# The gate of the context's recurrence ahead of the mLSTM half of its output projection, with four load buffers on ScalarE's queue

## The chip, the cores and the metric

The kernel runs on one core of one Trainium2 chip. A core has a matrix engine (TensorE, PE in the profile; PEld is its weight loading), VectorE (DVE), ScalarE (ACT), GpSimd (POOL) and SyncE (SP), which here only issues DMAs; the other engines can issue DMAs too. The metric is the device time of one execution in microseconds (us). The kernel before took 2059.33 us, the median of three runs (2057.45 to 2059.98).

## The reference

Two layers of a backbone over 512 latent tokens and 256 context tokens, width 1024, in f32. The change is in layer 0, whose mixer has two halves of 512 channels with one joint output projection:

```python
def rwkv_run(...):                    # both directions, context first, then latent
    def step(S, inp):                 # per token, 8 heads of 64
        sa = einsum('zbhij,zbhj->zbhi', S, a_t)
        S = S * w_t + sa * b_t + v_t * k_t
        return S, einsum('zbhij,zbhj->zbhi', S, r_t)
...
def rwkv_out(y, r, k, v, g, ...):
    yn = group_norm(y) * ln_w + ln_b
    return (yn + bonus(r, k, v)) * g  # the gate
...
oc = concatenate([mlstm_out(...), rwkv_out(...)]) @ out_w    # context's mixer output
h_ctx = h_ctx + gc1 * oc
h_ctx = h_ctx + gc2 * sq_relu_mlp(modulate(rms_norm(h_ctx), sc2, cc2), w1, w2)
```

The recurrence over the context ends in the state from which the one over the latent tokens starts.

## The kernel before

Activations lie with channels on partitions. A GEMM takes its f32 operands as two fp32r parts each: `xh`, `xl` of the activations (ScalarE casts, L280, VectorE subtracts, L281; `split_x`), `wh`, `wl` of the weights (ScalarE, L237; VectorE or GpSimd, L241), and adds the products xh·wh, xl·wh and xh·wl in one PSUM tile `psg`. One output tile of 128 channels over the 256 context tokens from 512 inputs has 12 matmuls; the result goes into the residual `res_c` on VectorE (L338).

The recurrence runs in 12 steps of 64 tokens, steps 0 to 3 the context and 4 to 11 the latent tokens, each step with its two directions. `step(s)` (L945) is the chain on the state: `psC<-X,AS`, `r`, `psC<-r,T`, `X`, then the new state `psC<-X,BK`, `S`, and the output `psC<-X,Q` and `psC<-S,ar`, which is added into `ya_c`. `pre(s)` (L842) prepares a step: it loads `ar`, `bk`, `AS`, `X` over SP, forms the products `psA`, brings the triangular blocks through DRAM (`dA`, `M`) into a form in which VectorE inverts them (`tm`, `Xi`, 15 pairs of instructions at L889 and L891), and back through DRAM (`invD`, `Xr`, and its transpose `Xt`, L899); from there four small products `psI` with `dd` (L909), `t` (L917, L919) and `d` (L930, ScalarE) lead to `T` (L938). `rwkv_norms` (L1007) normalises `ya_c` once step 3 is through (L995 to L1003).

The large GEMMs lie between these steps. The generator `fillers()` (L1113) gives them out in one order, and `pull` takes so many microseconds of them after each step (`PL`, L1131). Their order here is: the latent half of the input projection, the latent mLSTM half of the output projection, the context's mLSTM half (`ctx_mlstm`, L1042), and, once step 3 has set "ctx", `ctx_half` (L1058): the gate (`rwkv_gate`, L1013), its splits, the context's recurrence half of the output projection and the context's MLP. The gate moves `ya_c` through TensorE into `psy`, multiplies by the first half of `gb` (VectorE, L1023) and adds the second half (GpSimd, L1024) into `ro_c`, four times, for 128 channels each; `gb` comes from DRAM (`gD`) through two buffers. `moD` holds the context's mLSTM output in DRAM, loaded into `xlmc` and split there into `xhmc` and `xlmc`. What an engine runs when is set by a tile scheduler at build time; each engine then keeps its order. `Stats` and `rms` (`psst`, `psbc`, `rs`) form the norm ahead of the MLP, whose split input is `xh`, `xl`.

Of the kernel before, what the change touches and what calls it, by code (L numbers as in the profile page):

```python
# [11 lines left out]
F32 = mybir.dt.float32  # L12
# [6 lines left out]
P = 128  # L19
D = 1024  # L20
NK = D // P
CT = 256
# [95 lines left out]
def hybrid_kernel(ctx: ExitStack, tc: tile.TileContext, A, out):  # L118
    WS = [int(x) for x in "2222"]
    nc = tc.nc  # L120
    uid = [0]

    def nm(s):
        uid[0] += 1
        return f"{s}_{uid[0]}"
# [6 lines left out]
    def mm(o, l, r, start=True, stop=True, shared=False, tile=None):  # L132
        kw = {"tile_position": (32 * tile[0], 32 * tile[1])} if tile else {}
        return nc.tensor.matmul(o, l, r, start=start, stop=stop, skip_group_check=shared, **kw)  # L134
# [109 lines left out]
    def gemm(ap, xs, psp, both=0, k0=0, k1=NK, x0=0):  # L244

        w = split_w(ap[:, P * k0:P * k1], both)
        res = [gemm_w(w, x, psp, x0) for x in xs]
        bg[2] += bg[1]
        while bg[2] >= 1.0:
            bg[2] -= 1.0  # L250
            next(bg[0], None)
        return res
# [26 lines left out]
    def split_x(h, l, x):  # L279
        nc.scalar.copy(h, x)  # L280
        nc.vector.tensor_tensor(l, x, h.bitcast(F32), op=ALU.subtract)  # L281
# [55 lines left out]
    def add_gated(r_, ps, cnd, m, layer, idx):  # L337
        nc.vector.scalar_tensor_tensor(r_, ps, modcol(layer, idx, m, cnd), r_, op0=ALU.mult, op1=ALU.add)  # L338

    def out_proj(layer, cnd, res, x, k0, k1, psp, both, stats=None, x0=None):  # L340

        for m in range(NK):
            add_gated(res[:, m, :], gemm(A["out_w"][layer, m], [x], psp, both, k0, k1, k0 if x0 is None else x0)[0], cnd, m, layer, 2)
            if stats:
                stats.add(res[:, m, :])
            yield x[2] / 512 * 0.65 * (k1 - k0)
# [62 lines left out]
    xin = A["hT"]  # L409
    CTX, LAT = slice(0, CT), slice(CT, T)  # L410
    st_x = [ExitStack() for _ in SEGS]
    XN = [None, None]
    for i in (1, 0):
        n = SEGS[i][1]
# [3 lines left out]
    psg2 = st_f.enter_context(tc.tile_pool(name="psg2", bufs=2, space=PSUM, side="right"))  # L418
# [61 lines left out]
    gD = [pd.tile([P, 2, 4, n], F32, name=f"gD{n}") for _, n, _ in SEGS]  # L480
    moD = pd.tile([P, HM, T], F32, name="moD")
# [20 lines left out]
    with tc.tile_pool(name="pg1", bufs=1) as pg1:  # L502
# [20 lines left out]
        for z in range(2):  # L523
# [5 lines left out]
            m = pg1.tile([HM, T], F32, tag="mz", name=nm("m"))  # L529
# [483 lines left out]
    def rwkv_gate(si, dst, po, psp):  # L1013

        n = SEGS[si][1]
        for p in range(4):
            gb = po.tile([P, 2, n], F32, tag="gb", name=nm("gb"))
            nc.sync.dma_start(gb, gD[si][:, :, p, :])
            py_ = psp.tile([P, n], F32, tag="g", name=nm("psy"))
            for c in range(n // CR):  # L1020
                for q in range(2):
                    mm(py_[hs_[q], 64 * c:64 * c + 64], YA[si][hs_[q], c, p, :], id2[q])
            nc.vector.tensor_tensor(gb[:, 0], py_, gb[:, 0], op=ALU.mult)  # L1023
            nc.gpsimd.tensor_tensor(dst(p), gb[:, 0], gb[:, 1], op=ALU.add)  # L1024
# [5 lines left out]
    def lat_mlstm(res):  # L1030

        with tc.tile_pool(name="prm", bufs=1, side="right") as prm:
            xh = prm.tile([P, 4, LT], F32R, name="xhom")
            xl = prm.tile([P, 4, LT], F32R, name="xlom")
            for i in range(4):
                y = xl[:, i, :].bitcast(F32)
                nc.sync.dma_start(y, moD[:, i, LAT])
                split_x(xh[:, i, :], xl[:, i, :], y)
            for m in range(NK):
                nc.sync.dma_start(res[:, m, :], xin[:, m, LAT])  # L1040
            yield from out_proj(0, 0, res, (xh, xl, LT), 0, 4, psg2, WS[2])

    def ctx_mlstm():

        pres = st_c.enter_context(tc.tile_pool(name="pres", bufs=1, side="right"))
        res = RES["c"] = pres.tile([P, NK, CT], F32, name="res_c")
        wide[0] = st_w.enter_context(tc.tile_pool(name="wp2", bufs=1, side="right"))
        nc.sync.dma_start(res, xin[:, :, CTX])
        with tc.tile_pool(name="pcm", bufs=1, side="right") as pcm:
            xh = pcm.tile([P, 4, CT], F32R, name="xhmc")  # L1050
            xl = pcm.tile([P, 4, CT], F32R, name="xlmc")
            y = xl.bitcast(F32)
            nc.sync.dma_start(y, moD[:, :, CTX])
            split_x(xh, xl, y)
            yield from out_proj(0, 1, res, (xh, xl, CT), 0, 4, psg2, WS[2])

    def ctx_half():
        res = RES["c"]  # L1058
        with tc.tile_pool(name="pro", bufs=1, side="right") as pro, tc.tile_pool(name="po", bufs=2, side="right") as po:
            ro = pro.tile([P, 4, CT], F32, name="ro_c")  # L1060
            rwkv_gate(0, lambda p: ro[:, p, :], po, psg2)
            xh = pro.tile([P, 4, CT], F32R, name="xhoc")
            xl = pro.tile([P, 4, CT], F32R, name="xloc")
            for i in range(4):
                split_x(xh[:, i, :], xl[:, i, :], ro[:, i, :])
            stats = Stats(CT, po, psh2, "h")
            yield from out_proj(0, 1, res, (xh, xl, CT), 4, NK, psg2, WS[3], stats, 0)
            rb = stats.rms(psg2, "g")
        yield from mlp(0, 1, CT, res, 8, psg2, "right", WS[3], rb, 0)
        wide[0] = None  # L1070
        st_w.close()
# [45 lines left out]
    def fillers():  # L1117
        yield from rwkv_in(1, psg2, psh2, "h", st_x[1].close)
        done.add("in")
        RES["l"] = st_l.enter_context(tc.tile_pool(name="plr", bufs=1, side="right")).tile([P, NK, LT], F32, name="res_l")  # L1120
        yield from lat_mlstm(RES["l"])
        YA[1] = st_c.enter_context(tc.tile_pool(name="pyl", bufs=1, side="right")).tile([P, 8, 4, 64], F32, name="ya_l")
        done.add("lat")
        yield from ctx_mlstm()
        while "ctx" not in done:
            yield None
        yield from ctx_half()

    fill = fillers()
    PL = [18, 15, 21, 10, 21]  # L1130
    pull(fill, PL[0])  # L1131
# [18 lines left out]
    res = RES["l"]  # L1150
# [11 lines left out]
    with tc.tile_pool(name="prl", bufs=1) as prl, tc.tile_pool(name="pol", bufs=2) as pol:  # L1162
        ro = prl.tile([P, 4, LT], F32, name="ro_l")
        xh = prl.tile([P, 4, LT], F32R, name="xhol")
        xl = prl.tile([P, 4, LT], F32R, name="xlol")
        rwkv_gate(1, lambda p: ro[:, p, :], pol, psg3)
        pull(fill, 1e9)
        st_f.close()
        psg4 = st_q.enter_context(tc.tile_pool(name="psg4", bufs=2, space=PSUM, side="right"))
        psa3 = st_3.enter_context(tc.tile_pool(name="psa3", bufs=1, space=PSUM, side="right"))  # L1170
        for i in range(4):
            split_x(xh[:, i, :], xl[:, i, :], ro[:, i, :])
        stats = Stats(LT, pol, psg3)
        for _ in out_proj(0, 0, res, (xh, xl, LT), 4, NK, psg3, 0, stats, 0):
            pass
        rb = stats.rms()
# [15 lines left out]
    xh = px.tile([P, NK, LT], F32R, name="xh1")  # L1192
    xl = px.tile([P, NK, LT], F32R, name="xl1")
# [290 lines left out]
```

## Time and profile before

| | us |
|---|---|
| median of three runs | 2059.33 |
| lowest, highest | 2057.45, 2059.98 |
| the profiled execution | 2055.02 |
| its span | 2053.2 |
| TensorE busy | 1947.8 (95%) |
| VectorE, ScalarE, GpSimd busy | 1083.9, 874.3, 835.6 |

The mean granted clock of TensorE in this execution was 0.973. All times below are from the span's start. One execution is profiled; the time outside the span (1.8 us) is start and end. A timeline row has its start, how long it took, the line of the kernel, and in brackets how long the engine had been idle and what ended that. The clock of a stretch is given as a share of full speed: 1.00 is 2.4 GHz, 0.50 is 1.2 GHz.

### The profile page before, as it was taken

Reading aid. Unit: us, or ns where it says so; the run is one execution under the profiler, and the core shown is the slowest. Engines: PE = TensorE matmul, PEld = TensorE weight load, DVE = VectorE, ACT = ScalarE, POOL = GpSimd, SP = SyncE. Lnnn points to the kernel's source line nnn. Section 1 sums busy time; section 2 is a strip of 40 time slices with the busy share of each in tenths; the row PEclk is TensorE's granted clock in tenths of the full one; section 3 lists DMA queues with packets and bytes.
Section 4 is the critical chain, followed back from the end, with each engine's and each line's share of the span. In section 5 each row is a group of like instructions: output and inputs, shape, how many; then the busy total and the mean of one; then the engine's idle time right before and its main releaser. Section 6 shows DMA issues by size and latency. Waiting matters only on the chain. (4 is left out here: it accounts for less than half of the span.)

```text
span 2053.2 us, 36769 instructions
## 1 busy us (share of the span) xinstructions
PE 1947.8 (95%) x14924; PEld 1599.5 (78%) x14924; DVE 1083.9 (53%) x2087; ACT 874.3 (43%) x1441; POOL 835.6 (41%) x563
## 2 busy tenths in 40 slices
PE   6899998898897999999999999999999999999998
PEld 4788886666676899889787888888666678888887
DVE  6773645777878666776642221263666664122122
ACT  4444445354533444443433232343665654233232
POOL 1455555233432222224344444434454453444444
PEclk9999999998998999999999999999999999999999
DMA  7356557454585555544524332334111122333232
GB/s 303 107 197 218 176 203 263 123 152 111 166 249 152 124 171 159 146 134 135 210 93 133 94 101 93 101 111 141 59 52 34 57 75 82 103 94 102 93 103 72
DMA packets 171833, 271.62 MB, mean 132 GB/s; under 512 B 74960, under 2 KB 113488, under 8 KB 166544
## 3 DMA queue, kind: packets, MB, share of 16 engines
q1 hardware_dynamic: 166608, 263.76, 41.0%
q10 hardware_dynamic: 5056, 5.51, 0.8%
q8 instruction: 118, 1.93, 0.4%
q14 instruction: 51, 0.42, 0.1%
HBM read 244.06 MB, written 25.17 MB: 131 GB/s over the span
## 5 line engine op out<-in xcount | busy, mean ns | idle before, releaser
L241 POOL TENSOR_TENSOR wl<-w,wh 128x1024 fp32r<-128x1024 f32 (+3 forms) x252 | 573.5, 2278 | 851.5 <-PE psg L134 420.5
L237 ACT CAST wh<-w 128x1024 fp32r<-128x1024 f32 (+3 forms) x319 | 313.4, 985 | 517.5 <-PE psg L134 442.8
L134 PE MATMUL psg<-xh,wh 128*128 128x512 f32 (+1 forms) x1440 | 498.2, 361 | 13.3 <-DVE tm L889 6.5
L134 PE MATMUL psg<-xl,wh 128*128 128x512 f32 (+1 forms) x1440 | 496.5, 357 | 0.8 <-DVE xl L335 0.4
L134 PEld LDWEIGHTS psg<-xh,wh 128*128 128x128 f32 x1440 | 272.3, 190 | 68.3 <-issue 20.5
L134 PE MATMUL psg<-xh,wl 128*128 128x512 f32 (+1 forms) x1440 | 325.0, 356 | 0.0
L134 PEld LDWEIGHTS psg<-xl,wh 128*128 128x128 f32 x1440 | 274.4, 191 | 46.0 <-issue 7.6
L134 PEld LDWEIGHTS psg<-xh,wl 128*128 128x128 f32 x1440 | 242.0, 191 | 41.5 <-issue 7.0
L134 PE MATMUL psg<-hl,wh 128*128 128x512 f32 (+1 forms) x800 | 267.4, 348 | 0.9 <-DVE hl L281 0.9
L134 PE MATMUL psg<-hh,wh 128*128 128x512 f32 (+1 forms) x800 | 266.2, 349 | 1.2 <-DVE res_c L338 1.0
L338 DVE SCALAR_TENSOR_TENSOR res_l<-psg,mod,res_l 128x512 f32<-128x512 f32 (+1 forms) x108 | 74.1, 689 | 277.2 <-PE psg L134 277.2
L134 PEld LDWEIGHTS psg<-hh,wh 128*128 128x128 f32 x800 | 150.9, 189 | 22.5 <-issue 2.0
L134 PEld LDWEIGHTS psg<-hl,wh 128*128 128x128 f32 x800 | 151.2, 189 | 20.6 <-DVE hl L281 1.3
L134 PE MATMUL psg<-hh,wl 128*128 128x512 f32 (+1 forms) x800 | 164.6, 347 | 0.0
L383 DVE TENSOR_SCALAR r<-psg 128x512 f32<-128x512 f32 (+1 forms) x96 | 57.4, 600 | 176.9 <-PE psg L134 176.9
L134 PEld LDWEIGHTS psg<-hh,wl 128*128 128x128 f32 x800 | 131.6, 189 | 19.0
L281 DVE TENSOR_TENSOR hl<-r,hh 128x512 fp32r<-128x512 f32 (+1 forms) x96 | 90.0, 940 | 83.6 <-ACT hh L280 83.4
L384 ACT ACTIVATE r<-r 128x512 f32<-128x512 f32 (+1 forms) x96 | 53.5, 560 | 118.7 <-DVE r L383 118.7
L241 DVE TENSOR_TENSOR wl<-w,wh 128x1024 fp32r<-128x1024 f32 (+1 forms) x67 | 81.5, 1217 | 19.5 <-ACT wh L237 12.0
L889 DVE TENSOR_TENSOR tm<-M,Xi 64x15 f32<-64x15 f32 (+4 forms) x180 | 60.1, 334 | 23.5 <-DMA M<-dA 17.4
L134 PE MATMUL psada<-adaw,sc 128*32 128x256 f32 (+1 forms) x896 | 62.4, 383 | 8.3 <-DMA adaw<-in_ada_w_dram 4.2
L134 PE MATMUL psA<-ar,bk 64*128 64x128 f32 x384 | 55.2, 311 | 8.1 <-issue 3.6
(420 smaller groups left out, 2869.1 us busy)
## 6 DMA issues: line engine op xcount, KB each, us to landing
w<-in_w_dram SPq DMA_DIRECT2D x192, 512.0 KB, 3.6
adaw<-in_ada_w_dram SPq DMA_DIRECT2D x40, 1024.0 KB, 7.2
w<-in_ev_in_dram SPq DMA_DIRECT2D x47, 512.0 KB, 3.7
w<-in_od_in_dram SPq DMA_DIRECT2D x32, 512.0 KB, 3.6
adaw<-in_ada_dram SPq DMA_DIRECT2D x16, 512.0 KB, 11.2
w<-in_out_w_dram SPq DMA_DIRECT2D x32, 256.0 KB, 3.0
bk<-bkD SPq DMA_DIRECT2D x12, 512.0 KB, 4.7
ar<-arD SPq DMA_DIRECT2D x12, 512.0 KB, 4.8
```

Source lines behind the costliest of these rows:

```text
L134: return nc.tensor.matmul(o, l, r, start=start, stop=stop, skip_group_check=shared, **kw)
L237: nc.scalar.copy(wh, w)
L241: eng.tensor_tensor(wl, w, wh.bitcast(F32), op=ALU.subtract)
L281: nc.vector.tensor_tensor(l, x, h.bitcast(F32), op=ALU.subtract)
L338: nc.vector.scalar_tensor_tensor(r_, ps, modcol(layer, idx, m, cnd), r_, op0=ALU.mult, op1=ALU.add)
L383: nc.vector.tensor_scalar(r_, ps, 0.0, None, op0=ALU.max)
L384: nc.scalar.activation(r_, r_, AF.Square)
L889: nc.vector.tensor_tensor(t_, M[:, m:16, j:j + 1].to_broadcast([64, n, m]), Xi[:, j:j + 1, 0:m].to_broadcast([64, n, m]), op=ALU.mult)
```

## The change

`ctx_half` is now a generator `ctx_gate` in three parts. `ctx_mlstm` takes its first part ahead of its own loads: the four `gb` loads, each with a buffer of its own, issued by ScalarE. Then come the loads of `moD`, in four parts and on ScalarE's queue, each split by itself, and `res_c` in two loads on SP. The second part is the gate and the splits of its result, then the mLSTM half of the output projection, then the third part, the rest of what `ctx_half` was. `fillers()` waits for "ctx" ahead of all this, not between.

```diff
--- before.py
+++ after.py
@@ -1014,8 +1014,11 @@
 
         n = SEGS[si][1]
         for p in range(4):
-            gb = po.tile([P, 2, n], F32, tag="gb", name=nm("gb"))
-            nc.sync.dma_start(gb, gD[si][:, :, p, :])
+            if isinstance(po, list):
+                gb = po[p]
+            else:
+                gb = po.tile([P, 2, n], F32, tag="gb", name=nm("gb"))
+                nc.sync.dma_start(gb, gD[si][:, :, p, :])
             py_ = psp.tile([P, n], F32, tag="g", name=nm("psy"))
             for c in range(n // CR):
                 for q in range(2):
@@ -1045,24 +1048,36 @@
         pres = st_c.enter_context(tc.tile_pool(name="pres", bufs=1, side="right"))
         res = RES["c"] = pres.tile([P, NK, CT], F32, name="res_c")
         wide[0] = st_w.enter_context(tc.tile_pool(name="wp2", bufs=1, side="right"))
-        nc.sync.dma_start(res, xin[:, :, CTX])
+        gate = ctx_gate()
+        next(gate)
         with tc.tile_pool(name="pcm", bufs=1, side="right") as pcm:
             xh = pcm.tile([P, 4, CT], F32R, name="xhmc")
             xl = pcm.tile([P, 4, CT], F32R, name="xlmc")
             y = xl.bitcast(F32)
-            nc.sync.dma_start(y, moD[:, :, CTX])
-            split_x(xh, xl, y)
+            for i in range(4):
+                nc.scalar.dma_start(y[:, i, :], moD[:, i, CTX])
+                split_x(xh[:, i, :], xl[:, i, :], y[:, i, :])
+            for m in range(0, NK, 4):
+                nc.sync.dma_start(res[:, m:m + 4, :], xin[:, m:m + 4, CTX])
+            next(gate)
             yield from out_proj(0, 1, res, (xh, xl, CT), 0, 4, psg2, WS[2])
-
-    def ctx_half():
+        yield from gate
+
+    def ctx_gate():
+
         res = RES["c"]
         with tc.tile_pool(name="pro", bufs=1, side="right") as pro, tc.tile_pool(name="po", bufs=2, side="right") as po:
             ro = pro.tile([P, 4, CT], F32, name="ro_c")
-            rwkv_gate(0, lambda p: ro[:, p, :], po, psg2)
             xh = pro.tile([P, 4, CT], F32R, name="xhoc")
             xl = pro.tile([P, 4, CT], F32R, name="xloc")
+            gbs = [po.tile([P, 2, CT], F32, tag="gb", bufs=4, name=nm("gb")) for _ in range(4)]
+            for p in range(4):
+                nc.scalar.dma_start(gbs[p], gD[0][:, :, p, :])
+            yield 0.0
+            rwkv_gate(0, lambda p: ro[:, p, :], gbs, psg2)
             for i in range(4):
                 split_x(xh[:, i, :], xl[:, i, :], ro[:, i, :])
+            yield 0.0
             stats = Stats(CT, po, psh2, "h")
             yield from out_proj(0, 1, res, (xh, xl, CT), 4, NK, psg2, WS[3], stats, 0)
             rb = stats.rms(psg2, "g")
@@ -1121,10 +1136,9 @@
         yield from lat_mlstm(RES["l"])
         YA[1] = st_c.enter_context(tc.tile_pool(name="pyl", bufs=1, side="right")).tile([P, 8, 4, 64], F32, name="ya_l")
         done.add("lat")
-        yield from ctx_mlstm()
         while "ctx" not in done:
             yield None
-        yield from ctx_half()
+        yield from ctx_mlstm()
 
     fill = fillers()
     PL = [18, 15, 21, 10, 21]
```

In the order of TensorE's instructions the first place is the end of the latent mLSTM projection (`psg` from `xhom`). Before, this stands there; `psI` is the preparation of step 3, `xhmc` belongs to the context's mLSTM half, `psA` prepares step 4:

```order
L134 MATMUL psI_5956<-t_1060_5951,AB_5776 32x32 x16
L134 MATMUL psg_6708<-xhmc,wh_6704 128x256
L134 MATMUL psg_6708<-xlmc,wh_6704 128x256
...
L134 MATMUL psg_6708<-xhmc,wl_6706 128x256 x4
L134 MATMUL psA_6370<-ar_6359,bk_6360 128x128 x4
L134 MATMUL psA_6378<-ar_6359,bk_6360 128x128
L134 MATMUL psI_5975<-t_1059_5948,d_1063_5973 32x32 x16
```

and now, up to the first of the context's mLSTM GEMMs (`psy` is the gate, `psC` step 3 up to `psC_6314`, then step 4):

```order
L134 MATMUL psI_5956<-t_1060_5951,AB_5776 32x32 x16
L134 MATMUL psA_6370<-ar_6359,bk_6360 128x128 x4
L134 MATMUL psA_6378<-ar_6359,bk_6360 128x128 x4
L134 MATMUL psI_5975<-t_1059_5948,d_1063_5973 32x32 x16
...
L134 MATMUL psC_6314<-S_5722,ar_5772 64x64 x16
L134 MATMUL psC_6902<-X_6253,AS_6362 64x64 x16
L134 MATMUL psy_6729<-cst,ya_c 64x64 x8
L134 MATMUL psy_6740<-cst,ya_c 64x64 x8
L134 MATMUL psA_7008<-ar_6997,bk_6998 128x128 x4
...
L134 MATMUL psA_7024<-ar_6997,bk_6998 128x128 x4
L134 MATMUL psg_6787<-xhmc,wh_6783 128x256
```

The eight mLSTM GEMMs, which were spread over step 3 and the preparation behind it, have moved behind all of step 3 and behind the gate's `psy`.

The second place is ScalarE's order from the last weight cast of the latent projection to `d` of step 3, before and now in one piece:

```order
 L237 CAST wh_6663<-w_6661 128x512
+L1075 DMA gb_6702<-gD_583 128x2x256
+L1075 DMA gb_6703<-gD_583 128x2x256
+L1075 DMA gb_6704<-gD_583 128x2x256
 L923 ACTIVATE T_5953<-t_1059_5948,cst 128x8x32 x2
-L237 CAST wh_6704<-w_6702 128x512
-L280 CAST xhmc<-xlmc 128x1024
...
+L1075 DMA gb_6705<-gD_583 128x2x256
+L1058 DMA xlmc<-moD 128x256 x4
+L237 CAST wh_6783<-w_6781 128x512
...
 L930 COPY d_1063_5973<-psI_5956 128x128
```

Eight DMA issues have come ahead of `d`, and the split of `xlmc` has gone behind it.

The third place is TensorE behind the last gate GEMM of the context (`psg` from `xhoc`), up to the norm's `psbc`. Before, the rest of step 4 stood there (`psC_6842` to `psC_6883`), and step 5's `psI` with `Xr` came nine matmuls of the MLP later:

```order
L134 MATMUL psg_7418<-xhoc,wl_7416 128x256 x4
L134 MATMUL psC_6842<-r_6840,T_6540 64x64 x16
L134 MATMUL psst_7250<-cst,acc_7272 128x1 x2
L134 MATMUL psC_6861<-X_6253,BK_6416 64x64
L134 MATMUL psst_7250<-cst,sq_7432 128x1 x2
L134 MATMUL psC_6861<-X_6253,BK_6416 64x64 x15
L134 MATMUL psC_6883<-X_6253,Q_6361 64x64 x16
L134 MATMUL psC_6883<-S_6309,ar_6359 64x64 x16
L134 MATMUL psbc_7441<-cst,rs_7438 128x128 x2
```

and now:

```order
L134 MATMUL psI_7105<-Xr_7101,AB_7001 32x32 x16
L134 MATMUL psI_7105<-Xt_7103,AB_7001 32x32 x16
L134 MATMUL psg_7428<-xloc,wh_7424 128x256
L134 MATMUL psg_7428<-xhoc,wl_7426 128x256 x4
L134 MATMUL psC_7610<-X_6901,AS_7000 64x64 x12
L134 MATMUL psst_7260<-cst,acc_7282 128x1 x2
...
L134 MATMUL psI_7140<-Xt_7103,dd_7138 32x32 x16
...
L134 MATMUL psA_7716<-ar_7705,bk_7706 128x128 x4
...
L134 MATMUL psI_7181<-t_1234_7176,AB_7001 32x32 x16
L134 MATMUL psbc_7451<-cst,rs_7448 128x128 x2
```

Step 4 has gone ahead of the last gate GEMM, and the first three `psI` of step 5 and half its successor's `psA` have come ahead of `psbc`.

## Rows read from the trace of the kernel before

**Rows 1.** Windows: stretch, length, busy us of PE, PEld, DVE, ACT, POOL; clock, DMA.
```profile
589.94:639.24 49.30, 40.40 (x532) 36.56 (x521) 35.75 (x90) 18.84 (x37) 10.04 (x12) 0.83 0.69 197
649.94:680.00 30.06, 23.80 (x355) 20.74 (x355) 22.28 (x56) 10.57 (x22) 4.11 (x4) 0.72 0.44 107
639.24:649.94 10.70, 10.31 (x198) 9.72 (x198) 10.52 (x29) 6.63 (x13) 4.02 (x3) 1.00 0.67 203
```

**Rows 2.** Timeline of PE: start, duration, line, output<-inputs, count, [idle before, releaser].
```profile
588.57 1.07 PE L134 MATMUL psg<-xhom,wl 128*128 128x512 f32 x4
589.57 0.45 PE L134 MATMUL psI<-t,AB 32*32 32x32 f32 x32
591.96 0.38 PE L134 MATMUL psg<-xhmc,wh 128*128 128x256 f32 x1 [1.94 <-ACT xhmc L280]
...
597.33 0.45 PE L134 MATMUL psI<-t,d 32*32 32x32 f32 x32
...
598.80 0.28 PE L134 MATMUL psg<-xlmc,wh 128*128 128x256 f32 x1
598.92 0.28 PE L134 MATMUL psg<-xhmc,wh 128*128 128x256 f32 x1
```

**Rows 3.** Timeline of PE, the gate and the projection behind it.
```profile
633.80 0.55 PE L134 MATMUL psg<-xhoc,wh 128*128 128x256 f32 x1 [4.42 <-issue]
...
638.78 0.48 PE L134 MATMUL psI<-Xt,AB 32*32 32x32 f32 x32
...
649.88 0.64 PE L134 MATMUL psg<-xhoc,wl 128*128 128x256 f32 x4
```

**Rows 4.** Timeline of DVE, context norm, triangular inverses and gate.
```profile
611.88 0.41 DVE L889 TENSOR_TENSOR tm<-M,Xi 64x15 f32<-64x15 f32 x1 [0.93 <-DMA M<-dA]
...
614.39 0.67 DVE L1003 TENSOR_TENSOR ya_c<-ya_c,ms 128x512 f32<-128x512 f32 x1
...
630.28 0.17 DVE L891 TENSOR_TENSOR Xi<-Xi,tm 64x15 f32<-64x15 f32 x1
633.27 0.42 DVE L1023 TENSOR_TENSOR gb<-psy,gb 128x256 f32<-128x256 f32 x1 [2.83 <-DMA gb<-gD]
...
638.43 0.17 DVE L889 TENSOR_TENSOR tm<-M,Xi 64x15 f32<-64x15 f32 x1
...
661.42 0.17 DVE L891 TENSOR_TENSOR Xi<-Xi,tm 64x15 f32<-64x15 f32 x1
...
670.22 0.45 DVE L899 STREAM_TRANSPOSE Xt<-Xr 128x256 f32<-128x256 f32 x1 [1.47 <-DMA Xr<-invD]
```

**Rows 5.** Instructions of tile gb: duration ns min/median/max, starts; time to landing.
```profile
L1018 SPq DMA_DIRECT2D gb<-gD x4: 572/632/1118, 590.9 to 629.1; - x4
...
DMA to landing us min/median/max: 5.3/6.4/7.6
```

**Rows 6.** Timeline of PE: the same 16 psA at the two clocks.
```profile
483.17 3.09 PE L134 MATMUL psA<-ar,bk 64*128 64x128 f32 x16
...
615.33 1.71 PE L134 MATMUL psA<-ar,bk 64*128 64x128 f32 x16
```

**Rows 7.** Timeline of ScalarE before step 3's solve.
```profile
586.09 0.62 ACT L237 CAST wh<-w 128x512 fp32r<-128x512 f32 x1
...
592.86 0.25 ACT L930 COPY d<-psI 128x128 f32<-128x128 f32 x1
```

**Rows 8.** Timeline of PE from step 4's solve to step 5.
```profile
652.08 1.15 PE L134 MATMUL psC<-r,T 64*64 64x64 f32 x32 [1.56 <-DVE T L938]
...
657.44 1.86 PE L134 MATMUL psC<-X,BK 128*64 128x64 f32 x29 [1.58 <-DVE X L960]
...
662.31 0.71 PE L134 MATMUL psbc<-cst,rs 128*128 128x128 f32 x4
...
668.53 2.08 PE L134 MATMUL psA<-ar,bk 64*128 64x128 f32 x10 [1.48 <-DMA ar<-arD]
...
698.06 1.15 PE L134 MATMUL psC<-S,ar 64*64 64x64 f32 x32
```

## The prediction

> **What bounds the kernel now.** I read the windows first, because the page's shares are averages. From the end of the latent mLSTM projection to the end of the context's output projection, TensorE is not one long busy stretch [rows 1]: in 589.94:639.24 it works 40.40 of 49.30 us at a mean clock of 0.83, in 639.24:649.94 nearly all the time at 1.00, and in 649.94:680.00 23.80 of 30.06 us at 0.72. So 8.9 and 6.3 us are idle. At clock 0.83 some 8.4 us of the first stretch are missing (0.17 x 49.3), of which about 1.5 fall into idle time; likewise 8.4 less 1.8 in the last. Altogether the two stretches lose about 8.9 + 6.9 = 16 us and 6.3 + 6.6 = 13 us. Everywhere else TensorE is full and later work only shifts, so the change is priced by when TensorE gets through this region.
>
> Then TensorE's timeline. The last latent GEMM begins its tail at 588.57; after the `psI` at 589.57 the engine waits 1.94 us for ScalarE's split of `xlmc` [rows 2]. Eight mLSTM GEMMs of the context (12 matmuls each, 0.12 us apart at the full clock [rows 2], so 1.44 us) then lie between the pieces of recurrence step 3 until 620. The first GEMM on the gate's result begins at 633.80, after 4.42 us in which nothing runs [rows 3]. The reader should look at what ends that gap: VectorE's gate multiplication waits 2.83 us for `gb` [rows 4]. There are four such loads and two buffers, so the last is issued only at 629.1, when one came free, and a landing takes 5.3 to 7.6 us [rows 5]. That wait is what the four buffers remove.
>
> VectorE's timeline gives the other chain: `ya_c` is normalised at 614.39 + 0.67, the triangular inverse of the next step starts at 611.88 and ends at 630.28 + 0.17, TensorE uses its transposed result at 638.78 [rows 3, 4].
>
> **The change part by part.**
>
> Removed: the 4.42 us before the gate GEMMs and the half clock that follows idle TensorE there; the wait of 1.94 for the split of `xlmc` [rows 2, 3]. The load of `moD` in four and of `res_c` in two comes early beside other work: I cost it at nothing, since its reader now stands far behind. Without that cover it would cost one landing, 7.6 us by the slowest seen [rows 5].
>
> Added, first place: step 3 loses its cover. The order has no GEMM between `psI` and the end of step 3's `psC`. Before, eight GEMMs (11.5 us at the full clock) lay there. TensorE will be mostly idle from about 590 to 617, and what it has runs partly at the half clock: 16 `psA` took 3.09 us instead of 1.71 [rows 6].
>
> Added, second place: ScalarE's queue. Eight DMA issues and three casts now stand ahead of `d` (L930), which ran at 592.86 for 0.25 [rows 7]. The gate loads wait for semaphores of earlier transfers, so the first goes out near 587.0 and the last near 592 (an estimate: ScalarE's last cast before it starts at 586.09 [rows 7], and each following load waits for one of the landings of 5.3 to 7.6 us already under way). The first `moD` part waits for the first `gb` landing, 587.0 + 7.6 = 594.6. The other three (2 to 3 more) and three casts (0.62 each) bring `d` to 598.3–599.4, against 592.86. The `psI` that reads it stood at 597.33 [rows 2], so this costs the chain +1.8; with landings of 5.3 us it costs nothing, with a queue that fills up perhaps 4.
>
> From there to the normalised `ya_c` it took 615.06 - 597.33 = 17.7 us. The lower clock adds up to 4 (32 `psA`, eight transposes and three groups of 32 `psC`), the missing GEMMs and `res_c` additions on TensorE and VectorE take away up to 4. I take 617, between 614.4 and 618.8.
>
> Added, third place: the inverse now follows the first gate multiplication on VectorE, so it starts at 617 + 0.7 (`psy`) + 0.4 = 618.5, 6.6 later than 611.88. It is denser, because only one `res_c` addition stands in it: 30 small operations (0.17 to 0.41 in [rows 4], say 0.22), 6.6 us, four gate multiplications and four splits at 0.42, the evacuations of `psA` between them: 13 to 17, I take 15, against 18.6. It ends at 633.5, +3.0. With the same 8.3 us (630.45 to 638.78) to TensorE the `psI` starts at 641.8, +3.0.
>
> What is late next: at that point TensorE has four more GEMMs left to do than before (5.8 us). So the recurrence is 3.0 late, the GEMMs 8.8. Further, the order puts step 4's `psI` and parts of its `psC` between those GEMMs. The last gate GEMM, which ended at 650.5, I put at 666.5: 3.0 + 5.8, and 7.2 for step 4's pieces (1.15 at 652.08 and 4.9 from 657.44 to 662.31 for its `psC` groups [rows 8], the rest for the `psI` between).
>
> The same from the other side: step 5's inverse, which took 23.2 us (638.43 to 661.59 [rows 4]), starts behind `Xt` near 640.5 and has fewer additions of GEMMs still to wait for; its own work and what stands in it come to about 17 us, so it ends near 657.5. From its end to `Xt` it took 8.6 us, up to 670.22 [rows 4]; now 666. The first `psI` of step 5 stands inside the last gate GEMM, which agrees with 666.5.
>
> Given back: those pieces stood behind the last gate GEMM before, with waits. From 650.5 to the end of `psC<-S,ar` of step 5 (698.06 + 1.15) it took 48.7 us [rows 3, 8]. The way from the last GEMM to `psbc` took 11.8 (to 662.31); the waits of 1.56 and 1.58 for step 4 and the 4.9 of its `psC` leave it, and pieces of step 5 fill what the statistics leave idle. I put 8, so -4. Behind `psbc`, all sixteen `psA` (2.08 for ten, so 3.3), the wait of 1.48 for their `ar`, four groups of `psI` (0.45 to 0.65, so 2.2) and one idle microsecond or the half clock that follows leave: -8. That is 12 back of the 16. From step 5 on the order of both kernels is nearly the same, so the rest shifts unchanged.
>
> Sum: +16 - 12 = +4 us. The profiled execution took 2055.02 us (2053.2 its span), so 2059 for one like it; against the median of 2059.33, 2063. For this case alone I allow -1 to +9: `ya_c` at 614.4 takes 3 off and at 618.8 adds 2, the 12 may be 9 to 14.
>
> A queue of its own might seem to bring the loads quicker. The rows show up to 7.6 us from issue to landing for a `gb` load [rows 5], with many other loads in flight. The Trainium skill (DMA: Bandwidth & Descriptors, "Issuing engines are not separate DMA queues") says that transfers issued by any engine run on the same 16 DMA engines, and that several issuers save only the issuing time. By that rule the move to ScalarE saves SP about 0.65 us per load, off the path; the sum above stays. If the queue did speed the landing to 5.3, `d` would come 2.3 earlier and the sum would be about +2. The trace of before, where all these loads have SP's queue, cannot decide.
>
> **The rivals.**
> 1. *The gap goes and the chain keeps its pace: about -6 us, faster.* The gate loads land by 594, `d` isn't late, `ya_c` is ready at 613 and the inverse ends at 628.5. Then the last gate GEMM ends near 656.5, +6, and 12 come back. For it: the wait of 4.42 is real, VectorE and TensorE have less beside the chain, and step 3 before was stretched by GEMMs in its way. Against it: eight queue entries ahead of `d`, and a TensorE that idles at the half clock.
> 2. *The second gap isn't given back: about +11, slower.* It decides if step 5's inverse takes as long as before, 23.2 us, from 641: then `Xt` comes at 641 + 23.2 + 8.6 = 673, and since a late `Xr` now stops the last gate GEMM itself, this GEMM ends at 674 and not 666.5, with the same 36.6 behind it. For it: VectorE is busy through all of this stretch [rows 1], and `ar` was late once already [rows 8]. Against it: fewer GEMM results are left for VectorE to wait for.
> 3. *A wash, 0.* The gate GEMMs take a place in which TensorE would otherwise wait, and the gaps only change places: 16 us lost before in the first, 13 in the second [rows 1], the same sum after.
>
> **How the numbers follow.** Forecast 0.46, rival 1 0.27, rival 2 0.18, rival 3 0.09. A measurement of this kernel can't tell less than 0.2% (4.1 us) from no change. The forecast's own range straddles that bound, half each. So slower is 0.46/2 + 0.18 = 0.40, same 0.46/2 + 0.09 = 0.32, faster 0.27 and a little, 0.28. Range: 2059.33 - 8 to 2059.33 + 13, that is 2051 to 2072; the forecast's own is 2058 to 2068.
>
> **What would show it.** Right: TensorE idle for ten microseconds or more between 591 and 618 at a low clock; `d` near 598–599; the first L889 near 618 and the last L891 near 633; no gap of 4 us ahead of the gate GEMMs; the last gate GEMM near 666 and `psC<-S,ar` of step 5 ending near 703. Wrong: `d` before 595, or the last L891 before 630 (rival 1); waits for `Xr` or `ar` inside the last gate GEMM, and step 5 beyond 707 (rival 2). If step 5 ends where I say but the total differs, the later steps are not a mere shift, and the forecast fails there.

## The result, and the profile after

| | before | after |
|---|---|---|
| median of the runs side by side (7 each), us | 2060.08 | 2074.06 |
| lowest, highest | 2057.45, 2067.41 | 2069.68, 2078.16 |
| the profiled execution, its span | 2055.02, 2053.2 | 2069.89, 2068.1 |

The ratio is 1.0063, with a 95% interval of 1.0045 to 1.0080: 13 us slower (9 to 17). Slower is the side that had the largest chance, but I forecast +4, and the range ended 2 us below the median.

First the steps that came as written. TensorE's timeline after the last latent GEMM, whose tail begins at 588.02 and ends near 589.1:

```profile
588.02 1.07 PE L134 MATMUL psg<-xhom,wl 128*128 128x512 f32 x4
...
593.76 3.09 PE L134 MATMUL psA<-ar,bk 64*128 64x128 f32 x16 [4.29 <-DMA bk<-bkD]
598.78 0.65 PE L134 MATMUL psI<-t,d 32*32 32x32 f32 x32 [1.92 <-ACT d L930]
600.46 3.06 PE L134 MATMUL psA<-ar,bk 64*128 64x128 f32 x16 [1.03 <-DVE Q L863]
603.45 1.97 PE L134 MATMUL psC<-r,T 64*64 64x64 f32 x32
...
617.02 1.97 PE L134 MATMUL psy<-cst,ya_c 64*64 64x64 f32 x32 [4.40 <-DVE ya_c L1003]
...
641.72 0.45 PE L134 MATMUL psI<-Xr,AB 32*32 32x32 f32 x32 [0.88 <-DMA Xr<-invD]
```

Where [rows 2] had GEMMs between the small products, there are now gaps of 4.29, 1.92, 1.03 and 4.40 us, and all 32 `psA` run at the half clock (3.09 for 16, as in [rows 6]). `psI<-t,d` stands at 598.78 (forecast 599), step 4's `psI<-Xr` at 641.72; the `psI<-Xt` behind it, which the forecast counted from [rows 3], stands at 642.20 (forecast 641.8). VectorE's timeline agrees, beside [rows 4]:

```profile
616.27 0.69 DVE L1003 TENSOR_TENSOR ya_c<-ya_c,ms 128x512 f32<-128x512 f32 x1
618.52 0.17 DVE L889 TENSOR_TENSOR tm<-M,Xi 64x15 f32<-64x15 f32 x1
...
633.55 0.16 DVE L891 TENSOR_TENSOR Xi<-Xi,tm 64x15 f32<-64x15 f32 x1
```

Then it parts from the forecast. TensorE from the last gate GEMM to the MLP, answering [rows 8]:

```profile
669.05 0.45 PE L134 MATMUL psI<-Xr,AB 32*32 32x32 f32 x32 [2.17 <-DMA Xr<-invD]
...
670.14 0.66 PE L134 MATMUL psg<-xhoc,wl 128*128 128x256 f32 x4
...
676.12 3.09 PE L134 MATMUL psA<-ar,bk 64*128 64x128 f32 x16
...
679.73 1.22 PE L134 MATMUL psbc<-cst,rs 128*128 128x128 f32 x4
680.88 3.09 PE L134 MATMUL psA<-ar,bk 64*128 64x128 f32 x16
...
684.48 0.58 PE L134 MATMUL psg<-xh,wh 128*128 128x256 f32 x1
```

The last gate GEMM ends at 670.8, not 666.5, after a wait for `Xr` (rival 2's mark). From there 13.68 us pass to the first MLP GEMM, as many as before (650.52 to 664.18, 13.66). Before, TensorE waited in this stretch; now it is busy all through it, with small products at half clock:

```profile
670.80:684.48 13.68, 13.68 (x206) 12.43 (x205) 7.77 (x21) 5.84 (x15) 2.35 (x1) 0.50 0.43 123
```

The MLP thus starts 20 us late. Step 11 of the recurrence ends 13.3 late, and the profiled span is 14.9 longer.

The bill by stages: four stretches counted from the end of the latent projection in each kernel, first before, then after. I call length minus busy times clock the TensorE time lost.

```profile
589.64:629.64 40.00, 35.26 (x464) 31.53 (x464) 31.62 (x77) 16.47 (x32) 7.85 (x7) 0.89 0.74 219
629.64:669.64 40.00, 29.19 (x473) 26.52 (x474) 30.29 (x81) 16.06 (x33) 10.32 (x10) 0.80 0.61 157
669.64:699.64 30.00, 30.00 (x474) 27.61 (x474) 17.02 (x41) 14.34 (x27) 4.79 (x2) 0.85 0.37 101
699.64:739.64 40.00, 37.57 (x552) 35.05 (x552) 28.94 (x72) 17.59 (x30) 9.93 (x6) 1.00 0.59 160
```

```profile
589.09:629.09 40.00, 27.25 (x380) 24.92 (x380) 24.47 (x64) 14.04 (x31) 6.46 (x7) 0.70 0.58 171
629.09:669.09 40.00, 32.06 (x502) 30.03 (x503) 30.82 (x81) 14.27 (x29) 11.44 (x11) 0.91 0.58 156
669.09:699.09 30.00, 29.36 (x388) 26.80 (x389) 22.30 (x59) 15.35 (x31) 4.75 (x2) 0.72 0.41 120
699.09:739.09 40.00, 36.76 (x570) 34.69 (x570) 24.95 (x50) 16.86 (x31) 10.08 (x6) 0.96 0.53 157
```

Lost: 8.6, 16.7, 4.5, 2.4 before (32.2) and 20.9, 10.8, 8.9, 4.7 after (45.3). So 12.3 are paid in the first stretch, 5.9 come back in the second, and 4.4 and 2.3 are paid again: +13, as much as the result. Another profile of before's order (e4 below) loses 34.0 by the same count, so a difference of 2 us in such a bill says nothing. Counted in TensorE time, the give-back is what is lacking.

ScalarE's timeline, and a row of VectorE's, show what the loads do to the engines beside them [rows 7]:

```profile
585.09 4.41 ACTq L1075 DMA_DIRECT2D gb<-gD  x3
589.54 0.91 ACT L923 ACTIVATE T<-t,cst 128x256 f32<-128x256 f32 x2 [7.05 <-DMA w<-in_out_w_dram]
591.20 0.53 ACTq L1075 DMA_DIRECT2D gb<-gD  x1
592.27 4.54 ACTq L1058 DMA_DIRECT2D xlmc<-moD  x4
596.90 1.66 ACT L237 CAST wh<-w 128x512 fp32r<-128x512 f32 x3 [6.46 <-DMA gb<-gD]
598.47 0.25 ACT L930 COPY d<-psI 128x128 f32<-128x128 f32 x1
598.63 0.75 ACT L861 COPY AB<-psA 64x256 f32<-64x256 f32 x2
```

```profile
598.13 1.28 DVE L241 TENSOR_TENSOR wl<-w,wh 128x512 fp32r<-128x512 f32 x1 [8.25 <-ACT wh L237]
```

From 585.1 to 596.9 ScalarE computes for 0.91 us. The first `psA` are done on TensorE at 596.85, but ScalarE copies them away (L861) only at 598.63. VectorE waits 8.25 us for ScalarE's casts, and its own copies of `psA` (L862, L863) stand behind that subtraction; the second sixteen `psA` wait for `Q` (L863).

### The profile page after: what moved, and what is told of

It reads as the page before. It is cut to its first block, busy times and chain, and to the rows that moved or that the text cites. A ratio compares the mean times of both kernels' runs of the same rounds, so it can differ in the third digit from the quotient of the medians.

```text
span 2068.1 us, 36791 instructions
## 1 busy us (share of the span) xinstructions
PE 1951.8 (94%) x14924; PEld 1606.1 (78%) x14924; DVE 1090.4 (53%) x2090; ACT 873.8 (42%) x1444; POOL 836.1 (40%) x563
## 5 line engine op out<-in xcount | busy, mean ns | idle before, releaser
L241 DVE TENSOR_TENSOR wl<-w,wh 128x1024 fp32r<-128x1024 f32 (+1 forms) x67 | 79.6, 1188 | 27.1 <-ACT wh L237 19.2
L889 DVE TENSOR_TENSOR tm<-M,Xi 64x15 f32<-64x15 f32 (+4 forms) x180 | 54.9, 305 | 19.7 <-DMA M<-dA 14.5
```

What stands on the lines that cost most here:

```text
L241: eng.tensor_tensor(wl, w, wh.bitcast(F32), op=ALU.subtract)
L889: nc.vector.tensor_tensor(t_, M[:, m:16, j:j + 1].to_broadcast([64, n, m]), Xi[:, j:j + 1, 0:m].to_broadcast([64, n, m]), op=ALU.mult)
```

## The experiments

Each was timed beside the kernel before on the same chip; ratios are to that, with their 95% interval. Theory A: the lost cover of step 3 costs the time. Rival B: ScalarE's queue does.

**Order and queue apart.** e1 is the changed kernel with the eight loads on SP. e2 and e3 keep the old order (mLSTM GEMMs first, the gate after step 3) with the four buffers loaded early, e2 on ScalarE's queue, e3 on SP's.

```diff
# e1, e3 (against after)
-            for i in range(4):  nc.scalar.dma_start(y[:, i, :], ...
+            for i in range(4):  nc.sync.dma_start(y[:, i, :], ...
-                nc.scalar.dma_start(gbs[p], gD[0][:, :, p, :])
+                nc.sync.dma_start(gbs[p], gD[0][:, :, p, :])
# e2, e3: wait for "ctx" and next(gate) behind ctx_mlstm's out_proj
```

> The changed kernel with its eight loads (four gb, four of moD) back on SP's queue; order and buffers as changed. Theory A (step 3 has lost its GEMMs, TensorE stands idle and at the half clock, and the GEMM stream stays late): +9 to +14 us against the kernel before, at most 3 better than the changed kernel, because d (L930) comes earlier but nothing fills TensorE. Rival B (ScalarE's queue holds d back by 5.6 us and the whole chain with it): the loss falls to +4 to +8.

> The order of the kernel before (mLSTM GEMMs in step 3, gate behind them), with the four gb buffers, the early loads and ScalarE's queue of the changed kernel. Theory A: the gap of 4.42 us ahead of the gate GEMMs goes and nothing else is lost: -2 to -7 us against the kernel before. Rival B: d is late as in the changed kernel, so slower by +4 to +8.

> As e2_old_order_act, but all loads on SP's queue: the buffers and the early loads alone. Theory A: -2 to -7 us against the kernel before, like e2 within 3. Rival B: -2 to -7 as well, but at least 5 faster than e2.

| | SP's queue | ScalarE's queue |
|---|---|---|
| old order | e3 0.9959 (0.9941 to 0.9977) | e2 1.0028 (1.0007 to 1.0048) |
| gate first | e1 1.0003 (0.9983 to 1.0023) | after 1.0063 (1.0045 to 1.0080) |

Along each row the queue costs 0.60 to 0.69%, 12 to 14 us; down each column the order costs 0.35 to 0.44%, 7 to 9 us, against e3, which beats both kernels (2053.15). e1 itself came out below either expectation (+0.6 us, -3.5 to +4.7). e1's windows:

```profile
590.62:630.62 40.00, 31.06 (x380) 28.27 (x381) 26.57 (x76) 12.84 (x28) 4.42 (x5) 0.67 0.65 175
630.62:670.62 40.00, 33.77 (x644) 31.13 (x642) 28.61 (x73) 15.68 (x31) 11.58 (x11) 0.94 0.62 168
670.62:700.62 30.00, 28.38 (x357) 25.05 (x357) 25.54 (x72) 16.33 (x34) 4.75 (x2) 0.94 0.49 129
700.62:740.62 40.00, 38.66 (x600) 36.40 (x599) 22.29 (x42) 19.41 (x34) 11.14 (x7) 1.00 0.58 157
```

Lost: 19.2, 8.3, 3.3, 1.3, in sum 32.1, as before the change (32.2). The cover is lost here too (+10.6 in the first stretch), and 8.4, 1.2 and 1.1 come back. So A doesn't explain the 13 us: its loss is real, but is returned when the loads don't stand on ScalarE. ScalarE and TensorE of e1, from the end of the latent projection (590.6) on, then its way from the last gate GEMM to the MLP:

```profile
593.11 0.26 ACT L930 COPY d<-psI 128x128 f32<-128x128 f32 x1
596.57 0.36 ACT L861 COPY AB<-psA 64x256 f32<-64x256 f32 x1 [3.20 <-PE psA L134]
```

```profile
594.49 3.06 PE L134 MATMUL psA<-ar,bk 64*128 64x128 f32 x16 [3.49 <-DMA bk<-bkD]
597.49 0.65 PE L134 MATMUL psI<-t,d 32*32 32x32 f32 x32
598.06 3.09 PE L134 MATMUL psA<-ar,bk 64*128 64x128 f32 x16
601.09 1.97 PE L134 MATMUL psC<-r,T 64*64 64x64 f32 x32
...
635.48 0.45 PE L134 MATMUL psI<-Xr,AB 32*32 32x32 f32 x32 [0.82 <-DMA Xr<-invD]
...
663.91 0.45 PE L134 MATMUL psI<-Xr,AB 32*32 32x32 f32 x32 [2.82 <-DMA Xr<-invD]
...
676.12 1.71 PE L134 MATMUL psA<-ar,bk 64*128 64x128 f32 x16
...
678.49 0.39 PE L134 MATMUL psg<-xh,wh 128*128 128x256 f32 x1
```

```profile
670.85:678.49 7.64, 7.64 (x147) 6.79 (x147) 4.91 (x15) 4.51 (x12) 2.35 (x1) 1.00 0.76 203
```

Here the copy L861 waits for `psA`, not `psA` for the copy. Counted from the end of the latent projection, the changed kernel is later than e1 by 2.8 at `psI<-t,d` (9.7 against 6.9), 3.9 at `psC<-r,T`, 7.8 at step 4's `psI<-Xr` and 6.7 at step 5's; its MLP starts 7.5 later (95.4 against 87.9). The last gate GEMM ends only 1.5 later (81.7 against 80.2); the other 6.0 are lost on the way from there to the MLP, 13.68 us at clock 0.50 against 7.64 at 1.00. TensorE's order differs there, too: in e1 step 5's `psI<-Xr` stands in the last gate GEMM but one, so that a whole GEMM follows its wait of 2.82; in the changed kernel five matmuls follow the wait of 2.17. The order is set at build time, and no run here has SP's queue with the changed kernel's order.

**The order without its loads.** e12 has the changed order, but two buffers, the gate's loads in its loop, and `moD` and `res_c` each in one piece, on SP. e17 is e12 with the four early loads. e11 is the kernel before with four buffers and nothing else; e13 the old order with four buffers loaded early behind `moD`, on SP.

```diff
# e11 (against before)
-            gb = po.tile([P, 2, n], F32, tag="gb", name=nm("gb"))
+            gb = po.tile([P, 2, n], F32, tag="gb", bufs=2 if si else 4, name=nm("gb"))
# e12 (against after); e17 keeps gbs and its four loads, on SP
-            gbs = [po.tile(..., bufs=4, ...) for _ in range(4)]   # and its loads
-            rwkv_gate(0, lambda p: ro[:, p, :], gbs, psg2)
+            rwkv_gate(0, lambda p: ro[:, p, :], po, psg2)
```

> The kernel before with one edit: four gb buffers instead of two for the context's gate; order, moD load and queue (SP) as before. If the wait for a free buffer was the loss that could be had (4.42 us and the half clock behind it), the ratio is 0.995 to 0.998, as e3_old_order_sp (0.9959) or a little better, since d, bk and the moD load keep their places. If e3's gain came from the split of the moD load, 1.000.

> The changed order alone: gate ahead of the mLSTM half, with two buffers, moD in one piece, res_c in one piece, all loads on SP's queue. From the four kernels of orders and queues the order costs 7 to 9 us; without the four buffers the gate's third and fourth loads come late again, and they now stand ahead of the mLSTM GEMMs: ratio 1.003 to 1.007. If the order is free and only its combination with early loads cost, 1.000.

> Old order, four buffers, SP's queue, as e3_old_order_sp, but the gb loads stand behind the moD load (in one piece): TensorE's first mLSTM GEMM should start near 593 and not 601, and the time be at or below e3: ratio 0.993 to 0.996. If that start does not matter, 0.996 as e3.

> Between e12_order_only (1.0064) and e1_gate_first_sp (1.0003): the changed order with four gb buffers loaded early on SP, but moD and res_c in one piece each. If the late gb loads made the difference, 1.000 to 1.002; if the moD load in parts did, 1.005 to 1.007.

Measured: e11 1.0005 (0.9982 to 1.0028), e12 1.0064 (1.0038 to 1.0089), e13 0.9966 (0.9941 to 0.9991), e17 0.9999 (0.9987 to 1.0012). With two buffers the order costs 13 us against before, and four early loads return all of it: with two buffers the last gate load goes out at 630.6. `moD` and `res_c` in parts are worth nothing (e17 against e1; e13, with `moD` in one piece, gains like e3).

e11 is the surprise. TensorE's timeline, for the gap of [rows 3] and later:

```profile
630.88 0.58 PE L134 MATMUL psg<-xhoc,wh 128*128 128x256 f32 x1 [0.19 <-DVE gb L1023]
...
656.39 0.58 PE L134 MATMUL psg<-xh,wh 128*128 128x256 f32 x1 [0.59 <-ACT xh L334]
...
670.32 0.45 PE L134 MATMUL psI<-Xr,AB 32*32 32x32 f32 x32 [2.50 <-DMA Xr<-invD]
```

The 4.42 us have gone and the MLP starts 7.8 earlier than before (664.18), yet the time is the same: the GEMMs run ahead, the recurrence doesn't follow, and TensorE waits for `Xr` behind them. So filling the visible gap was worth nothing here. Whether it was slack, or its gain was eaten by step 4, whose `psI<-Xr` comes 5.7 later than before (644.20 against 638.50), is open.

**How much cover.** e4 moves only the wait for "ctx" ahead of the mLSTM half; e5 puts four of the eight mLSTM GEMMs ahead of the gate, loads on SP.

```diff
# e4 (against before)
-        yield from ctx_mlstm()
         while "ctx" not in done:
             yield None
+        yield from ctx_mlstm()
# e5 (against e1), in ctx_mlstm
+            for _ in range(4):
+                yield next(half)
+            while "ctx" not in done:
+                yield None
             next(gate)
-            yield from out_proj(...)
+            yield from half
```

> The kernel before with one edit: the mLSTM half of the context's projection waits for the end of step 3, too; the gate stays behind it, two buffers, SP's queue. Theory A: nearly the whole loss, +9 to +16 us against the kernel before. Rival B, and a rival C (the gate's multiplication ahead of the inverse on VectorE is what delays step 4): about 0 to +4, as neither is in this kernel.

> Loads on SP's queue, four buffers; of the eight mLSTM GEMMs four come ahead of the wait for step 3, then the gate, then the other four. If the price of the order is step 3's lost cover (about 9 us between the two orders on SP's queue, ratios 0.9959 and 1.0003), half the cover gives half of it or more: 0.995 to 0.998. If it is the gate standing ahead of the inverse on VectorE, this kernel keeps it: 0.999 to 1.001.

e4: 0.9998 (0.9978 to 1.0019). It was no test of A: the scheduler moved the GEMMs forward again, and each engine had the order of before. It serves as a measure of single profiles: its profiled execution took 2064.80 us, that of before 2055.02, for the same instructions. e5: 1.0015 (0.9999 to 1.0031); half the cover gains nothing on e1, which speaks against A again. The other side of that expectation, the gate standing ahead of the inverse on VectorE, lies nearer (0.999 to 1.001) and has no test of its own.

**The queue taken apart.** Against after: e8 has only the `gb` loads on ScalarE's queue, e9 only the `moD` loads, e14 all eight on GpSimd's; e10 lets VectorE copy `d`.

```diff
# e10
-        nc.scalar.copy(d1, pi)
+        nc.vector.tensor_copy(d1, pi)
```

> The changed kernel with the four moD loads on SP's queue, the four gb loads still on ScalarE's. Theory B1 (what costs is the chain on ScalarE's queue: a moD load waits for the landing of a gb load, and casts, d and the evacuations of psA stand behind): d at about 593.5 instead of 598.5, ratio to before 1.000 to 1.002, against 1.0063 of the changed kernel. Rival B2 (every load on ScalarE's queue costs its share): half of it, 1.003 to 1.0045.

> The other half: gb loads on SP's queue, the four moD loads on ScalarE's. Theory B1: d at about 593 to 595, ratio 1.000 to 1.002. Rival B2: 1.003 to 1.0045. With both halves near 1.000 the cost is not additive, and with both near 1.003 it is.

> The changed kernel with the copy d (L930) on VectorE, in all steps; the loads stay on ScalarE's queue. If d is what the queue holds up (theory B3), psI<-t,d comes near 597 and at least 6 of the 12 us come back: ratio 1.003 or less. If it is the rest behind the queue (casts of the weights, evacuations AB of psA; theory B4), at most 3 us come back: 1.0045 to 1.0065.

> The changed kernel with its eight loads on GpSimd's queue instead of ScalarE's. If what stands behind the loads on ScalarE's queue is the cost (casts, evacuations of psA, d), this is like SP's queue: 0.999 to 1.002, d near 593. If any second queue costs (transfers in each other's way, landings later), 1.004 to 1.007.

e8 1.0049 (1.0031 to 1.0067), e9 1.0026 (1.0003 to 1.0049), e14 1.0034 (1.0011 to 1.0056), e10 1.0050 (1.0024 to 1.0075). Each half of the loads costs by itself, and the two sum roughly to the whole; GpSimd's queue costs half of it. B1 gave each half at most 1.002: e8 lies above that, e9's interval covers it. e14 lies between its two expectations. In e10 `d` is ready 0.7 us after the latent projection's end (592.08), but its timelines, ScalarE and then TensorE, show that the rest is as late as ever:

```profile
600.74 1.66 ACT L237 CAST wh<-w 128x512 fp32r<-128x512 f32 x3 [6.14 <-DMA gb<-gD]
602.30 0.75 ACT L861 COPY AB<-psA 64x256 f32<-64x256 f32 x2
```

```profile
604.29 3.06 PE L134 MATMUL psA<-ar,bk 64*128 64x128 f32 x16 [3.00 <-DVE Q L863]
607.29 1.97 PE L134 MATMUL psC<-r,T 64*64 64x64 f32 x32
```

`psC<-r,T` starts 15.2 after that end, against 14.4 in the changed kernel. So freeing `d`, the one reader that I had priced, returns little: the casts and the copies of `psA` behind the same entries are as late. But late copies aren't the whole price either. In e8, whose latent projection ends at 592.07, L861 waits for `psA` as in e1. Its step 5 even has `psI<-Xr` earlier, 68.5 after that end (e1: 73.3), and its last gate GEMM ends at 670.73, 78.7 after (e1: 80.2). Still e8 is some 9 us slower than e1. ScalarE, then TensorE:

```profile
599.70 0.36 ACT L861 COPY AB<-psA 64x256 f32<-64x256 f32 x1 [0.84 <-PE psA L134]
```

```profile
676.08 0.60 PE L134 MATMUL psst<-cst,acc 128*128 128x1 f32 x4 [4.18 <-DVE acc L308]
...
676.94 3.09 PE L134 MATMUL psA<-ar,bk 64*128 64x128 f32 x16
...
689.52 0.58 PE L134 MATMUL psg<-xh,wh 128*128 128x256 f32 x1
```

From its last gate GEMM to the MLP it takes 18.8 us, with a wait of 4.18 for the norm's sum and then the half clock. So what the variants off SP's queue share isn't one late reader. e9 and e10, whose TensorE order from the last gate GEMM to the MLP is the changed kernel's, take 13.7 us at 0.50 there, with `d` late or not; e14 takes 7.4 at 1.00, and its loss lies elsewhere. That points at the order on this way, but no run changes it alone.

**Another explanation.** The half clock around the norm could come from the norm meeting step 5's small products by accident; more GEMMs handed out after step 3 would then move it. e15 does that to the changed kernel, e16 to e1.

```diff
-            pull(fill, PL[4])
+            pull(fill, PL[4] + (10.4 if s == 3 else 0.0))
```

> The changed kernel with 10.4 us more GEMM work handed out behind step 3 (four GEMMs of the MLP), so that the stream of GEMMs stands to the recurrence as in the kernel before. If the missing give-back comes from GEMMs that now stand one step later in the program, at least half of the 13 us come back: ratio 1.000 to 1.003. If it comes from what happens inside step 3 and the gap around the norm (late evacuations on ScalarE, the half clock), it stays at 1.005 to 1.007.

> The same with the loads on SP's queue (e1_gate_first_sp had 1.0003). If alignment of GEMMs and recurrence is a loss of its own, better than e1: 0.995 to 0.998. If not, 0.999 to 1.003.

1.0088 (1.0063 to 1.0113) and 1.0064 (1.0039 to 1.0088): both slower, and above what was expected either way. The queue costs less here than elsewhere (0.24%), with intervals that overlap. This doesn't settle the question. By the bill of four stretches e15 loses 39.0, 6.3 less than the changed kernel; it loses 9.3 instead of 2.8 in the 50 us from 889.1 on. The edit gave some of the time back around the norm and paid it later, so an accident of place isn't excluded.

## Why the prediction was wrong, point by point

- *Step 3 loses its cover, `ya_c` at 617, the inverse from 618.5 to 633.5, `psI` at 641.8*: right to half a microsecond (616.96, 618.52, 633.7, 642.20). The 618.5 is partly luck: 617 + 0.7 + 0.4 is 618.1, and `psy` took 1.97 at the half clock, not 0.7.
- *`d` at 598.3 to 599.4, costing the chain +1.8*: the instant was right (598.47), the price wrong, and **this is the step that failed.** With the loads on SP (e1) 12 us come back, in the old order 14 (e2 against e3). I followed one entry behind the queue, `d`, to one reader; e10 frees `d` and returns at most 3 us (1.0050 against 1.0063, intervals overlap). The recurrence's lag on e1 grows from 2.8 at `psI<-t,d` to 7.8 at step 4's `psI<-Xr` (6.7 at step 5's), and most of the MLP's lag comes behind that, at the half clock ahead of the MLP.
- *16 up front, 12 given back, then a mere shift*: by the forecast's own marks it was 20.3, 12.3 and then 5.3 more, in sum +13.3. Up front, the last gate GEMM ends at 670.8 (before at 650.52); e1 pays nearly as much (19.3 counted from the latent projection's end, here 20.8), so most of this error is the order's. The 12 are there where I looked for them, at the end of `psC<-S,ar` of step 5 (707.2, +8.0), but not in the GEMMs: from the last gate GEMM to the MLP nothing comes back (13.68 us against 13.66; e1 takes 7.64). All 32 `psA` stand on this way and take 2 x 3.09 us, where 16 take 1.71 at the full clock [rows 6]. Nor is the rest a mere shift: step 6 ends only 4.6 later than before, but some 40 matmuls of the MLP fewer stand ahead of it (0.12 us each, so about 5 us); step 7 ends 12.4 later, step 11 13.3 (938.73 before, 952.01 after).
- *Without the queue's 1.8 the forecast was +2*: e1 measures +0.6 (-3.5 to +4.7). The order's sum was right, in part by luck, since e1 pays more up front and gets more back; the queue was priced at a seventh of its cost.
- *The 4.42 us before the gate GEMMs, removed, are a gain*: not borne out by e11 (1.0005).
- *Rivals*: 1 falls. 2 named the place (`Xr` late in the last gate GEMM) and nearly the size, +11, but by luck: it asked for a step 5 inverse of 23.2 us, and that took 16.2 (643.78 to 660.0), as forecast; e1 waits for `Xr` even longer (2.82) and loses nothing by it. 3 describes e1, not this kernel.
- *ScalarE's queue doesn't make the loads quicker*: right. The `gb` loads took 7.3 to 8.6 us from issue to landing in the changed kernel and 7.1 in e1, beside 5.3 to 7.6 before [rows 5].

The Trainium skill's rule (DMA: Bandwidth & Descriptors, "Issuing engines are not separate DMA queues"), that all issuers share the same 16 DMA engines, agrees with these landings. The same page of the Trainium skill ("Anatomy of one DMA — SWDGE (gpsimd) path") says that a DMA's semaphore wait happens on the issuing sequencer before dispatch; ScalarE's timeline agrees, where three `gb` issues of at most 0.59 us each span 4.41 us.

Shown is that moving the loads to ScalarE costs 12 to 14 us, in either order. How it does so is open: by what stands behind the loads, or by TensorE's order around the norm, which changes with the queue. Open too: why the clock stays at half around the norm with the loads on ScalarE but not in e1; why GpSimd's queue costs half; and why e3 and e13 beat e11, though the gap is gone in all three (e3's and e11's intervals don't overlap, e13's and e11's do).

## What to carry to other kernels

Before moving a DMA that must wait for a semaphore to a computing engine, list every instruction behind it up to the next one that waits anyway, and follow each to the next step of the chain, not to its first reader alone; here the move cost 0.6%. Compare the other engines' orders as well, since a move of loads can change them. Before counting a visible TensorE gap as a gain, see whether another chain is the later one at the next place where the two meet: in e11 filling it was worth nothing. Buffers, order and queue arrived as one change and don't simply add up: the order costs 0.64% with two buffers and 0.44% beside e3, early loads into four buffers return 0.65% in the new order and 0.3 to 0.4% in the old one, and the queue costs 0.60 to 0.69%. Test them apart.

## What was not expected of the hardware

TensorE can be fully busy and still at half clock. In the changed kernel, after the wait of 2.17 us, it is busy for 13.68 of 13.68 us at 0.50 (1.2 GHz) with small products of the recurrence and of the norm; it is at the full 2.4 GHz again after the MLP's GEMMs have begun. Small products alone don't explain it: in e1 the 32 `psA` and the norm's products run at 1.00, in 7.64 us. And one profile of the same instruction order can differ by 9.8 us from another (e4), so that differences in the end of a single trace below that say little.
